# A rarely taken path's DMAs issued from GpSimd instead of SyncE, and another order for four of the last pair's products

## The chip, the cores and the metric

The kernel runs on one core of a Trainium2 chip. The metric is the device time of one execution in microseconds (us). The time is about 1.8 us longer than the span that the profile shows; the span runs from the program's first instruction to its last. A ratio below is the mean time of one kernel's fast runs over the mean of the other's fast runs of the same rounds (in the experiments without the first, profiled run of each), so it is not quite the ratio of the medians that are quoted next to it. Differences between two experiments of the same rounds are differences of the means of six runs each; a "±" behind one is half the width of a 95% interval worked out from the scatter of those runs.

## The reference

```python
def setup_inputs():
    batch, seq, dim, hidden = 16, 256, 512, 2048
    return {
        "x": np.random.randn(batch, seq, dim).astype(np.float32),
        "w1": np.random.randn(dim, hidden * 2).astype(np.float32),
        "w2": np.random.randn(hidden, dim).astype(np.float32),
    }

def reference(x, w1, w2):
    h = x @ w1
    gate, value = np.split(h, 2, axis=-1)
    h = np.maximum(gate, 0) * value
    return (h @ w2).astype(np.float32)
```

## The kernel before

The kernel has two ways. The fast way computes in fp16, with seven products in place of eight (a Strassen-like scheme, P1 to P7), and meanwhile checks that the size of the inputs suits fp16. Only if they do not suit is the general way run afterwards, under a branch. The inputs drawn here suit, so the general way stands in the program but is never executed. Every engine still has to branch over it.

```python
    with ExitStack() as fast:
        unfit = fast_way(fast, tc, x2, w1, w2, out2, flag)
    with tc.If(unfit > 0, label="general"):
        with ExitStack() as general:
            general_way(general, tc, x2, w1, w2, out2)

def general_way(ctx, tc, x2, w1, w2, out2):
    # ... (pools, identity)
    for k in range(NK):
        for j in range(0, 2 * H, 1024):
            t = xp.tile([P, 1024], F32, name="g_t", tag="g_t")
            nc.sync.dma_start(out=t, in_=w1[k * P:(k + 1) * P, j:j + 1024])
            # ... (three more dma_start like it: w2, x, and the output)
```

In the fast way, the second matrix product of the last of four passes is done in pairs of row blocks. The last pair (number 3) is what remains at the very end. Each of its products is eight matmuls. After P1, ScalarE copies the sum from bank X to bank Y. After P5 and P6 it moves W and Y to `pu`; P2 and P4 end in ScalarE copies to the output tile, P7 and P3 in VectorE additions. Each of P2, P7, P3 and P4 of the last pair then sends a quarter of the pair's output, 128 KB, from SyncE.

```python
        def send(self, h, c):
            nc.sync.dma_start(out=out_v[self.s, h, self.t, :, c], in_=self.o[:, h, c])
        # ...
        def P2(self):
            self.o = tmp.tile([P, 2, DO], F32, name="o", tag="tmp")
            nc.scalar.activation(self.o[:, 0, :DO // 2], self.X, COPY, scale=1 / GS)
            if self.end:
                self.send(0, slice(0, DO // 2))
        # ...
        def P4(self):
            nc.scalar.activation(self.o[:, 1, :DO // 2], self.Y, COPY, scale=1 / GS)
            self.send(1, slice(0, DO // 2 if self.end else DO))
    # ...
    LAST_ORDER = ORDER.replace("P5 3, P2 3, P6 3, P3 3, P7 3", "P2 3, P6 3, P5 3, P7 3, P3 3")
    # ... (in the last pass)
            job(84, lambda: tc.mark_branch_hint_location("general", "LikelyTaken", [ENG.PE, ENG.DVE, ENG.SP]))
```

`ORDER` ends in "P1 3, P4 2, P5 3, P2 3, P6 3, P3 3, P7 3, P4 3"; the numeral after the product is the pair.

## Time and profile before

| | before |
|---|---|
| time, median of the first 3 runs | 309.0 us (308.88 to 310.2) |
| span of the profiled run | 307.5 us |
| TensorE busy | 300.7 us, 98% |
| last ScalarE copy begins | 302.97 us |
| last output DMA lands | 305.81 us |
| end of the span | 307.46 us |

From the page of the profile: the span, TensorE's line of the table of busy times, and the chain of work that ended last.

```profile
span 307.5 us, 5285 instructions
...
PE 300.7 (98%) x1905; PEld 184.0 (60%) x1905; DVE 235.9 (77%) x388; ACT 176.4 (57%) x348; POOL 151.4 (49%) x189
...
PE 96%; DMA 1%; SPq 0%; POOL 0%; ACT 0%; issue 0%
```

TensorE is what bounds the kernel. A change that leaves its work alone can only win at the two ends. The end begins as follows (timeline; columns: start us, length us, engine, line, operation, tiles):

```profile
302.97 0.39 ACT L405 ACTIVATE o<-Y 128x256 f32<-128x256 f32 x1 [2.23 <-PE Y L362]
303.38 1.07 SPq L370 DMA_DIRECT2D out_dram<-o  x1
```

The issue of that last output DMA occupies SyncE for 1.07 us; the view of the output tensor for the last three sends (minimum, median and maximum of the issue in ns; then the time from issue to landing) shows that 0.33 us is normal:

```profile
L370 SPq DMA_DIRECT2D out_dram<-o x3: 332/332/1072, 301.7 to 303.4; - x3
...
DMA to landing us min/median/max: 1.7/2.4/2.7
```

The same view for the last send alone:

```profile
DMA to landing us min/median/max: 2.4/2.4/2.4
```

What the sequencers did at the branch over the general way (the view of source line 42; columns: durations in ns, first and last start in us):

```profile
L42 SPq EVENT_SEMAPHORE  x8: 17/17/17, 305.0 to 305.8; - x8
...
L42 PEldq COMPARE_BRANCH  x1: 496/496/496, 301.8 to 301.8; - x1
...
L42 SPq COMPARE_BRANCH  x1: 73/73/73, 304.5 to 304.5; - x1
```

And at the end of the launch (view of source line 785):

```profile
L785 SPq EVENT_SEMAPHORE  x13: 17/28/28, 305.9 to 307.4; - x13
```

So SyncE, which has nothing left to do but wait for its DMAs, runs eight waits after its branch, the eighth held by the last landing at 305.81, and only then starts on the eleven waits of the launch end (the other two of the thirteen belong to the closing barriers). Those eleven take 0.062 us each.

In the 1.2 us from 302.9, the table of DMA queues has an instruction fetch of 16 KB (columns: packets, MB, share of 16 engines' time) among the packets of the output. The records of single packets put its start at 303.06 and its length at 1.01 us:

```profile
q8 instruction: 1, 0.02, 5.3%
```

### The profile page before, as it was taken

The page shows a single profiled execution, that of the slowest core. Times are in us where ns is not written, and L with a number is a line of the kernel's source. Part 1 is how long each engine was busy: PE and PEld are TensorE (multiplying, and loading weights), DVE is VectorE, ACT ScalarE, POOL GpSimd, SP SyncE. Part 2 cuts the span into 40 slices and gives each one's busy share as a digit, 9 for nine tenths or more (in the row PEclk, how much of TensorE's full clock was granted, in tenths as well). Part 3 has the DMA queues.
Part 4 walks back from the last instruction along what each step waited for, and adds up shares of the span by engine and source line. Part 5 has one row for each costly group of instructions (what it writes and reads, how often), then busy time and mean ns, then how long its engine had stood idle before and what let it go on. Part 6 is the DMA issues. An engine that isn't in the chain of part 4 may idle for free.

```text
span 307.5 us, 5285 instructions
## 1 busy us (share of the span) xinstructions
PE 300.7 (98%) x1905; PEld 184.0 (60%) x1905; DVE 235.9 (77%) x388; ACT 176.4 (57%) x348; POOL 151.4 (49%) x189
## 2 busy tenths in 40 slices
PE   7999999999999999999999999999999999999994
PEld 6844444588844444478864444458884444448883
DVE  2579888899768888887438888889536888888841
ACT  2488886455865555538845555546865555553231
POOL 2389999800069899200029889700007998700000
PEclk9999999999999999999999999999999999999998
DMA  6976779964765260001354910000335110001132
GB/s 207 357 257 190 227 177 174 225 123 87 270 193 86 69 136 3 0 0 67 136 175 103 207 34 2 0 2 24 115 108 167 35 34 0 3 1 34 53 120 74
DMA packets 35837, 32.88 MB, mean 107 GB/s; under 512 B 14432, under 2 KB 31328, under 8 KB 35680
## 3 DMA queue, kind: packets, MB, share of 16 engines
q1 hardware_dynamic: 33536, 26.22, 28.0%
q0 software_dynamic: 2272, 6.29, 11.4%
q8 instruction: 16, 0.26, 0.4%
q14 instruction: 13, 0.11, 0.1%
HBM read 27.26 MB, written 12.58 MB: 130 GB/s over the span
## 4 chain that ended last, share of the span: by engine, by line
PE 96%; DMA 1%; SPq 0%; POOL 0%; ACT 0%; issue 0%
PE Y L250 26%; PE X L250 17%; PE W L250 17%; PE Y L362 14%; PE X L362 9%; PE W L362 9%; DMA w_stage<-in_w_dram 1%; PE X L325 1%; PE W L325 1%; PE Y L325 1%; PE Y L498 0%; PE X L498 0%; SPq L488 0%; PE Y L154 0%; POOL w_B L466 0%; ACT o L405 0%
## 5 line engine op out<-in xcount | busy, mean ns | idle before, releaser
L250 PEld LDWEIGHTS <-w_T 128*128 128x128 f16 x496 | 48.3, 98 | 57.3 <-POOL w_T L232 1.1
L179 POOL TENSOR_TENSOR fold<-xh 128x1024 f32<-128x1024 f16 x16 | 30.3, 1894 | 94.5 <-DMA xh<-x 93.7
L250 PE MATMUL X<-x_A,w_B 128*128 128x512 f16 x248 | 73.8, 379 | 0.0
L250 PE MATMUL Y<-x_S,w_T 128*128 128x512 f16 x220 | 65.5, 379 | 0.0
L250 PEld LDWEIGHTS <-w_B 128*128 128x128 f16 x372 | 36.4, 98 | 42.0
L277 DVE SCALAR_TENSOR_TENSOR cc<-W,pu 128x512 f32<-128x512 f32 x62 | 42.9, 691 | 21.2 <-ACT pu L271 20.4
L257 ACT COPY Y<-X 128x512 f32<-128x512 f32 x62 | 35.4, 571 | 38.2 <-PE X L250 37.9
L271 ACT ACTIVATE pu<-Y 128x512 f32<-128x512 f32 x62 | 37.1, 598 | 33.9 <-PE Y L250 32.9
L182 POOL TENSOR_TENSOR fold<-fold 128x512 f32<-128x512 f32 (+2 forms) x96 | 51.8, 539 | 7.5
L362 PEld LDWEIGHTS <-w_stage 128*128 128x128 f16 x512 | 50.0, 98 | 5.8
L287 DVE SCALAR_TENSOR_TENSOR cc<-Y,pu 128x512 f32<-128x512 f32 x62 | 42.9, 691 | 6.7
L282 DVE SCALAR_TENSOR_TENSOR g<-X,cc 128x512 f16<-128x512 f32 x62 | 42.8, 691 | 2.3
L299 DVE SCALAR_TENSOR_TENSOR g<-Y,cc 128x512 f16<-128x512 f32 x62 | 42.2, 681 | 1.8 <-PE Y L250 1.8
L362 PEld LDWEIGHTS <-g 128*128 128x128 f16 x384 | 37.6, 98 | 8.2
L264 ACT ACTIVATE pu<-W 128x512 f32<-128x512 f32 x62 | 37.2, 600 | 0.8 <-PE W L250 0.6
L250 PE MATMUL W<-x_S,w_B 128*128 128x512 f16 x124 | 36.9, 379 | 0.0
L250 PE MATMUL W<-x_S,w_T 128*128 128x512 f16 x124 | 36.9, 379 | 0.0
L250 PE MATMUL Y<-x_A,w_T 128*128 128x512 f16 x124 | 36.9, 379 | 0.0
L362 PE MATMUL X<-w,g 128*128 128x256 f16 x256 | 31.9, 273 | 0.0
L394 DVE SCALAR_TENSOR_TENSOR o<-W,pu 128x256 f32<-128x256 f32 x16 | 6.8, 422 | 19.8 <-PE W L362 19.8
L169 DVE TENSOR_TENSOR w_stage<-g 128x1024 f16<-128x1024 f16 x32 | 21.4, 683 | 0.2
L232 POOL TENSOR_TENSOR w_T<-w_stage 128x512 f16<-128x512 f32 (+1 forms) x16 | 18.7, 1177 | 2.5 <-DMA w_stage<-in_w_dram 2.5
(100 smaller groups left out, 306.2 us busy)
## 6 DMA issues: line engine op xcount, KB each, us to landing
w_stage<-in_w_dram SPq DMA_DIRECT2D x14, 512.0 KB, 6.2
out_dram<-o SPq DMA_DIRECT2D x26, 256.0 KB, 2.1
x<-in_x_dram POOLq DMA_DIRECT2D x4, 1024.0 KB, 9.0
xh<-x SPq DMA_DIRECT2D x16, 256.0 KB, 3.0
w<-in_w_dram POOLq DMA_DIRECT2D x2, 1024.0 KB, 10.2
out_dram<-o SPq DMA_DIRECT2D x12, 128.0 KB, 1.7
w_stage<-in_w_dram SPq DMA_DIRECT2D x4, 256.0 KB, 5.4
x_S<-in_x_dram SPq DMA_DIRECT2D x4, 256.0 KB, 6.1
```

The source lines that it names most:

```text
L169: eng.tensor_tensor(o[n], o[i0], o[i1], op=op)
L179: nc.gpsimd.tensor_tensor(fold, t, t, op=MULT)
L182: nc.gpsimd.tensor_tensor(fold[:, :, :m], fold[:, :, :m], fold[:, :, m:2 * m], op=ADD)
L250: nc.tensor.matmul(ps, wop[wn][:, b, self.jb * P:(self.jb + 1) * P], self.xo[xn][:, b, :], start=fresh and b == 0, stop=b == 1, skip_group ...
L257: nc.scalar.copy(out=self.Y, in_=self.X)
L264: nc.scalar.activation(self.p5, self.W, COPY, scale=GS)
L271: nc.scalar.activation(self.u2, self.Y, COPY, scale=GS)
L277: nc.vector.scalar_tensor_tensor(out=self.c12, in0=self.W, scalar=GS, in1=self.u2, op0=MULT, op1=ADD)
L282: nc.vector.scalar_tensor_tensor(out=self.g[:, self.jb, :TH], in0=self.X, scalar=0.0, in1=self.c12, op0=MAX, op1=MULT)
L287: nc.vector.scalar_tensor_tensor(out=self.c22, in0=self.Y, scalar=GS, in1=self.p5, op0=MULT, op1=ADD)
L299: nc.vector.scalar_tensor_tensor(out=self.g[:, self.jb, TH:], in0=self.Y, scalar=0.0, in1=self.c22, op0=MAX, op1=MULT)
L362: nc.tensor.matmul(ps, self.op[an][:, i], vop[wn][:, i], start=name in ("P1", "P5") and i == 0, stop=i == NJ // 2 - 1, skip_group_check=True)
```

## The change

The diff tells two intents, which I infer. First, if the general way's DMAs belong to GpSimd, the skip path need not raise SyncE's eight DMA semaphores, and SyncE is the engine that ends last. Second, P7's result and its send come earlier, and P2's later, in the last pair. The diff, with the repeated lines of its first part cut:

```diff
-            nc.sync.dma_start(out=t, in_=w1[k * P:(k + 1) * P, j:j + 1024])
+            nc.gpsimd.dma_start(out=t, in_=w1[k * P:(k + 1) * P, j:j + 1024])
 ... (the same in the general way's loads of w2 and x and its store of the output)
@@ class Pair
-            self.s, self.t = s, t
+            self.s, self.t, self.o = s, t, None
+        def outputs(self):
+            if self.o is None:
+                self.o = tmp.tile([P, 2, DO], F32, name="o", tag="tmp")
         def P2(self):
-            self.o = tmp.tile([P, 2, DO], F32, name="o", tag="tmp")
+            self.outputs()
         def P7(self):
+            self.outputs()
@@
-    LAST_ORDER = ORDER.replace("P5 3, P2 3, P6 3, P3 3, P7 3", "P2 3, P6 3, P5 3, P7 3, P3 3")
+    LAST_ORDER = ORDER.replace("P5 3, P2 3, P6 3, P3 3, P7 3", "P6 3, P5 3, P7 3, P2 3, P3 3")
```

## The prediction

> **What bounds the kernel now.** TensorE. The page gives PE 300.7 us busy of a 307.5 us span (98%) at a granted clock of 0.996, and the chain of waits puts 96% of the span on PE. At the end (timeline, and the records of the lines of the branch and of the launch end): the last pair's products run back to back, 0.87 us per eight matmuls, until about 302.9; ScalarE copies P4 to `o` (302.97 to 303.36); SyncE issues the last output DMA at 303.38. That issue takes 1.07 us instead of the usual 0.33, and overlaps a 16 KB instruction fetch at 303.06. It lands at 305.81. SyncE branches at 304.50, goes on at 305.03, and runs eight semaphore waits of the skip path (about 0.08 us each), the eighth held by the landing to 305.83. Then come eleven waits of the launch end, 305.90 to 306.52, 0.062 us each, and two barriers to 307.46.
>
> **What the change does.**
>
> 1. General way. It is not executed with these inputs. But the skip path has to raise every semaphore that the general way would have raised. Before, SyncE does this for its eight DMA semaphores, each after waiting for its own DMA, so the eleven waits of the launch end can't start before the last landing. After (instruction order of the built kernel), SyncE's skip path has none, GpSimd has five instead, and the launch end has twelve waits on SyncE, the last on the last DMA's semaphore. So eleven run while that DMA is in flight, from about 304.7 to 305.4. Saved after the landing: 306.58 (the drain that follows) minus about 305.90, or 0.68 us, all on the critical path.
>
> 2. SyncE's own jump. It now jumps over one instruction instead of 187. The Trainium skill, "Runtime: NRT & Kernel Launch", Instruction fetch mechanics, says that a taken branch to a target outside the fetched window waits for a fetch. The trace agrees in part: 0.46 us after SyncE's branch against 0.13 on ScalarE, which jumps over one instruction. I expect 0.3 us less, hidden under the landing: worth nothing alone. GpSimd's jump gets long instead, at 289.5, 14 us before it matters.
>
> 3. Last pair's order. PE work is the same; P1, P3 and P4 keep their places. P6 moves before P5, and needs Y's copy (296.91 to 297.27) at 297.5: 0.25 us of slack. P7 needs P6's eviction (0.39 us) within P5's 0.87 us. P7's send moves from 301.74 to about 300.9, P2's from 299.0 to about 301.6. P3's and P4's stay at 302.55 and 303.38. Worth 0 to 0.1 us either way.
>
> **Predicted time.** 309.0 - 0.68 = 308.3 us; 8 in 10 between 307.8 and 308.9. Faster by over 2%: 1%; within 2%: 98%; slower: 1%.
>
> **What would show each step.** Step 1: the launch-end waits of SyncE begin near 304.7, the last ends within 0.05 us of the last landing, and the end comes about 1.0 us after it, against 1.65. Step 2: SyncE's first record after its branch comes within 0.2 us. Step 3: no idle PE between the last pair's products; the last issue stays at 303.4 with 1.07 us, if the instruction fetch still falls at 303.06.
>
> **What would make it wrong.** If the last issue were not slowed by the fetch, the landing would come 0.7 us earlier and the gain reach 1.3 us. If another engine's fetch delays the last landing (a fetch made one part of the send at 302.55 land 1 us late), the gain is lost. If the order makes PE wait, it costs some tenths. Run-to-run spread (308.88 to 310.2) is as large as the gain.

## The result, and the profile after

| | before | after |
|---|---|---|
| median of 6 runs | 309.47 us (308.88 to 310.2) | 308.99 us (308.08 to 309.99) |
| ratio | 1 | 0.9984, 95% interval 0.9959 to 1.0009 |
| start of last copy to end of span | 4.49 us | 4.33 us |
| start of last copy to last landing | 2.84 us | 3.37 us |
| last landing to end of span | 1.65 us | 0.96 us |

The measured time is 0.09 us above the predicted range. The difference is 0.48 us of medians where 0.68 was predicted, and it is not clear of noise. The same lines of the changed kernel, page first:

```profile
span 307.6 us, 5283 instructions
...
PE 301.0 (98%) x1905; PEld 183.9 (60%) x1905; DVE 235.9 (77%) x388; ACT 176.3 (57%) x348; POOL 151.3 (49%) x189
...
PE 96%; DMA 2%; SPq 1%; issue 0%; ACT 0%
```

The timeline of the end, and the last four sends in the view of the output tensor:

```profile
303.26 0.38 ACT L410 ACTIVATE o<-Y 128x256 f32<-128x256 f32 x1 [1.36 <-PE Y L362]
303.67 0.33 SPq L374 DMA_DIRECT2D out_dram<-o  x1
```

```profile
L374 SPq DMA_DIRECT2D out_dram<-o x4: 332/332/332, 301.2 to 303.7; - x4
...
DMA to landing us min/median/max: 1.7/2.3/3.5
```

The 3.5 us belong to the send before the last, which also landed before the last did (at 306.32). The view for the last send alone, and the instruction fetch in the table of DMA queues from 303.4 to 305.4:

```profile
DMA to landing us min/median/max: 3.0/3.0/3.0
```

```profile
q8 instruction: 1, 0.02, 4.6%
```

The branch (line 42) and the launch end (now line 790):

```profile
L42 POOLq EVENT_SEMAPHORE  x5: 17/43/43, 290.3 to 290.6; - x5
...
L42 PEldq COMPARE_BRANCH  x1: 1736/1736/1736, 301.2 to 301.2; - x1
...
L42 SPq COMPARE_BRANCH  x1: 68/68/68, 304.1 to 304.1; - x1
```

```profile
L790 SPq EVENT_SEMAPHORE  x14: 17/28/28, 304.3 to 307.5; - x14
```

What was meant to happen did. SyncE has no wait on line 42, its launch-end waits begin at 304.3 instead of 305.9, and the end comes 0.96 us after the landing instead of 1.65.

But 0.53 us of this was given back: the last landing came later after the copy. The last issue is no longer slow (0.33 us), yet the DMA lands 2.96 us after it. Its sixteen parts, read from the semaphore's updates: fourteen between 305.18 and 305.34, one at 305.62, one at 306.63. The Trainium skill, "DMA: Bandwidth & Descriptors", Why a DMA increments its semaphore by 16 and not by 1, says that a DMA's parts finish independently on up to 16 engines and that only the full 16 means that all data landed. The trace agrees: the wait ended at 306.64, with the sixteenth. By the packet records a 16 KB instruction fetch began at 303.66 (before: 303.06), within 0.01 us of the last issue, and took 1.46 us.

And TensorE's branch, which the prediction had left out, began at 301.21 instead of 301.79, although the last copy was 0.29 us later, and took 1.74 us instead of 0.50.

### The profile page after: what moved, and what is told of

Its sections match the earlier page's. It is cut to its first block, busy times and chain, and to the rows that moved or that the text cites. A ratio compares the mean times of both kernels' runs of the same rounds, so it can differ in the third digit from the quotient of the medians.

```text
span 307.6 us, 5283 instructions
## 1 busy us (share of the span) xinstructions
PE 301.0 (98%) x1905; PEld 183.9 (60%) x1905; DVE 235.9 (77%) x388; ACT 176.3 (57%) x348; POOL 151.3 (49%) x189
## 4 chain that ended last, share of the span: by engine, by line
PE 96%; DMA 2%; SPq 1%; issue 0%; ACT 0%
PE Y L250 26%; PE X L250 17%; PE W L250 17%; PE Y L362 14%; PE W L362 9%; PE X L362 9%; DMA x_S<-in_x_dram 2%; PE X L325 1%; PE W L325 1%; PE Y L325 1%; SPq L493 0%; PE Y L503 0%; SPq L217 0%; PE X L503 0%; ACT o L410 0%
```

## The experiments

Theory A: the saved waits are the gain; the new order spoils part of it, because it moves TensorE's branch and the instruction fetch behind the branch onto the last output DMA. Theory B: the order does nothing and where the fetch falls is chance. Four rounds of experiments were made on three chips; times of "before" of the same rounds are given with each round.

All traces together first. Times are us from the start of the last ScalarE copy, read from the records of single instructions, packets and semaphore updates; "fetch 1" and "fetch 2" are starts of the last 16 KB fetches before and after TensorE's branch begins.

| kernel | TensorE's branch: start, length | fetch 1 | fetch 2 | last issue | last landing | end |
|---|---|---|---|---|---|---|
| before | -1.18, 0.50 | -4.60 | 0.09 | 1.07 | 2.84 | 4.49 |
| e13 before again | -1.18, 0.50 | -4.45 | 0.07 | 1.15 | 2.93 | 4.58 |
| e1 general way only | -1.18, 0.50 | -4.08 | 0.09 | 1.00 | 2.79 | 3.75 |
| e12 the same again | -1.17, 0.50 | -4.04 | 0.07 | 0.97 | 2.75 | 3.72 |
| after | -2.05, 1.74 | -3.00 | 0.40 | 0.33 | 3.37 | 4.33 |
| e3 after again | -2.05, 1.58 | -2.99 | 0.25 | 0.33 | 3.11 | 4.07 |
| e10 after, third | -2.05, 1.96 | -2.65 | 0.62 | 0.33 | 3.43 | 4.40 |
| e2 order only | -2.05, 1.84 | -3.00 | 0.50 | 0.33 | 3.41 | 5.06 |
| e14 the same again | -2.06, 1.70 | -2.72 | 0.37 | 0.33 | 3.06 | 4.71 |
| e4 after, short general way | -2.05, 1.80 | -2.95 | 0.50 | 0.34 | 2.99 | 3.95 |
| e5 after, shifted by 62 | -2.06, 0.41 | -6.58 | -0.71 | 0.48 | 2.46 | 3.43 |
| e9 the same again | -2.05, 0.42 | -6.69 | -0.71 | 0.33 | 2.11 | 3.07 |
| e15 order only, shifted by 62 | -2.05, 0.41 | -6.63 | -0.71 | 0.56 | 2.41 | 4.06 |
| e6 general way only, shifted by 62 | -1.18, 0.41 | -6.65 | 0.17 | 0.33 | 2.92 | 3.88 |
| e7 general way only, shifted by 217 | -1.18, 4.44 | none near | -0.15, 3.99 | 1.76 | 3.64 | 4.60 |
| e8 no branch | none | -4.68 | none | 0.33 | 2.11 | 3.07 |
| e11 e5 without TensorE's hint | -2.05, 3.52 | -6.66 | -1.05, 2.20 | 0.39 | 2.37 | 3.33 |

### First round: the parts alone, and a shorter jump

Before: mean of 11 runs 309.37 us, median 309.4.

**e1**, only the general way's DMAs from GpSimd:

```diff
-            nc.sync.dma_start(out=t, in_=w1[k * P:(k + 1) * P, j:j + 1024])
+            nc.gpsimd.dma_start(out=t, in_=w1[k * P:(k + 1) * P, j:j + 1024])
 ... (and the other three)
```

> Only the general way's DMAs from GpSimd; the last pair keeps its old order. Theory A (the saved waits are the whole gain, the new order spoils part of it by moving TensorE's branch and its 16 KB instruction fetch onto the last output DMA): the span ends 0.95 to 1.0 us after the last landing (before 1.65), the last landing 2.8 to 2.9 us after the start of the last ScalarE copy, and the time is 0.6 to 0.8 us below before, ratio about 0.9978. Theory B (the order does nothing; where the fetch falls is chance): same end, the landing anywhere between 2.4 and 3.4 us after the copy, the time 0.4 to 0.7 us below before and the same as the full change within 0.3 us.

Measured: median 308.22 us, mean 308.20, ratio 0.996 (0.9942 to 0.9978). The end came 0.96 us after the landing, and the landing 2.79 us after the copy, both as theory A had it. The gain in time, 1.16 us, is larger than either theory had it and than the 0.74 us that the trace shows at the end (4.49 to 3.75); the repetition e12 below gives 0.66.

**e2**, only the new order:

```diff
-    LAST_ORDER = ORDER.replace("P5 3, P2 3, P6 3, P3 3, P7 3", "P2 3, P6 3, P5 3, P7 3, P3 3")
+    LAST_ORDER = ORDER.replace("P5 3, P2 3, P6 3, P3 3, P7 3", "P6 3, P5 3, P7 3, P2 3, P3 3")
 ... (and the helper `outputs`)
```

> Only the last pair's new order; the general way's DMAs stay on SyncE. Theory A: the branch of TensorE and the fetch that follows it fall as in the changed kernel (branch begun 0.6 us earlier than before and taking over 1 us, the fetch beginning within 0.1 us of the last issue), one part of the last DMA lands 1 us late, and the time is 0.3 to 0.6 us above before, ratio about 1.0015. Theory B: the time is that of before within 0.3 us, ratio 0.999 to 1.001. In both, the end comes 1.65 us after the last landing.

Measured: median 309.34 us, mean 309.36, ratio 0.9998 (0.9981 to 1.0016). The trace is theory A's in every point (branch, fetch, landing 3.41, end 5.06), but the time is theory B's. This was the one contradiction left, and e14 and e15 were made for it.

**e3**, the changed kernel again, without an edit:

> The changed kernel once more, as the partner of the other three and for a second trace. Theory A: the 16 KB fetch at TensorE's branch falls again within 0.1 us of the last issue and one part lands about 1 us late (last landing 3.3 us after the start of the last copy); time 0.3 to 0.6 us above the kernel with the general way's DMAs moved alone. Theory B: the fetch falls elsewhere by some tenths, and the landing changes with it; same time as the kernel with the DMAs moved alone. Both: 0.4 to 0.7 us below before.

Measured: median 308.62 us, mean 308.80, ratio 0.9982 (0.9964 to 1.0). In the same rounds e1 was faster by 0.60 ± 0.40 us. The full change is slower than half of it. The fetch began 0.17 us before the last issue rather than within 0.1, and the landing was 3.11.

**e4**, a general way with one chunk in place of eight, so that TensorE jumps over some 210 instructions instead of 1698:

```diff
-    for c in range(T // TH):
+    for c in range(1):
```

> The changed kernel, with a general way that handles one chunk of eight only (never executed here, wrong for inputs that need it): TensorE jumps over some 210 instructions instead of 1698, and VectorE over fewer too. If the fetches at the branch are what delays the last DMA, they move or vanish, the last landing comes 2.1 to 2.4 us after the start of the last copy instead of 3.37, and the time falls 0.4 to 1.0 us below the full change. If the length of the jump does not matter, nothing changes (within 0.2 us).

Measured: median 309.01 us, mean 308.96, ratio 0.9985 (0.9967 to 1.0004); against e3 no gain. The fetch after the branch was still there, at 0.50. So the length of the jump is not what matters here, and this guess was a miss.

### Second round: moving the fetch without touching the order

In e1 to e4 the order and the time of the fetch change together. The two fetches come from TensorE's instruction stream. The Trainium skill, "Runtime: NRT & Kernel Launch", Instruction fetch mechanics, says that instructions are refilled in blocks of 16 KiB, or 256 instructions, and that the next block is fetched while the current one executes. The traces agree: the fetches on queue 8 are of 16384 bytes, and the shifts below moved them. So empty instructions in TensorE's stream, spread over the kernel, move the block boundaries and leave the order of products and sends as it is.

Before: mean of 11 runs 309.54 us, median 309.24.

**e5**, the changed kernel with one empty instruction after the first product of each of the 62 blocks:

```diff
             self.mm("P1", self.X, True)
+            for _ in range(1):
+                nc.tensor.nop(hint="shift", nofuse=True)
```

> The changed kernel with 62 empty instructions in TensorE's stream (one after each first product of a block), which move its last instruction-block boundary 62 instructions earlier. Fetch theory (in the new order TensorE enters its last block so late, at 3.0 us before the last copy, that its branch waits 1.44 us after that fetch and the next fetch falls on the last output DMA): the first fetch begins 4 us or more before the copy, the branch takes about 0.5 us instead of 1.6 to 1.8, the second fetch begins at about -0.8 us, the last issue takes 0.33 us and the last landing comes 2.1 to 2.5 us after the start of the copy instead of 3.1 to 3.4; time 0.6 to 1.2 us below the full change and 0.2 to 0.7 below the general-way-only kernel, 307.5 to 308.0. Rival (the late landing belongs to the new order of the output DMAs, not to the fetch): landing stays at 3.1 or more and the time at 308.7 to 309.

Measured: median 307.9 us, mean 307.97, ratio 0.9944 (0.9924 to 0.9964). With the order of products and sends unchanged, the branch took 0.41 us, fetch 2 came at -0.71, and the landing at 2.46 us (the last issue took 0.48 us where 0.33 was expected). The rival, that the order of the sends makes the landing late, falls.

**e6**, the control: the same edit to e1.

> Control: the same 62 empty instructions in the kernel with only the general way's DMAs moved (old order). The branch there already takes 0.50 us, so both theories expect no change: branch at -1.18 us, second fetch at 0.1, last issue about 1.0 us, landing 2.8, time 308.0 to 308.4. If the empty instructions themselves cost or gain time, it shows here.

Measured: median 308.61 us, mean 308.57, ratio 0.9965 (0.9944 to 0.9986). A near miss in two points: fetch 2 came 0.1 us later than in e1, so the last issue was not slowed, but one part of the DMA landed late instead (2.92). The time is a little above the expected range. The empty instructions as such show no gain (e1 had 308.20, though in the round before and not side by side). One thing more can be read here: e5 and e6 have the same shift and differ in the order alone, and e5 is faster by 0.60 ± 0.49 us (from copy to end 3.43 against 3.88). With fetch 1 early in both, at -6.6, the new order is the better one, because its branch comes 0.87 us earlier and fetch 2 with it (-0.71 against 0.17).

**e7**, the old order with 217 empty instructions (three after each P1, one more after P5 of every other block), which is 39 short of a whole block of 256:

```diff
             self.mm("P1", self.X, True)
+            for _ in range(3):
+                nc.tensor.nop(hint="shift", nofuse=True)
 ...
             self.mm("P5", self.W, True)
+            if self.jb % 2:
+                nc.tensor.nop(hint="shift", nofuse=True)
```

> Old order, general way's DMAs moved, with 217 empty instructions, which is 39 short of a block of 256: the last block boundary falls later than in the old order without them. Fetch theory: the harm of the new order appears without it: first fetch at -3.2 to -2.1 us, the branch takes over 0.7 us and ends about 1.44 us after that fetch, the second fetch falls at or after the last issue (0.2 to 1.2 us), that issue takes 0.33 us and one part lands late, last landing 2.9 to 3.5 us after the copy; time 0.2 to 0.7 us above the general-way-only kernel. Rival (the order of the DMAs does it): landing 2.8, same time as the general-way-only kernel.

Measured: median 308.97 us, mean 309.03, ratio 0.9981 (0.996 to 1.0003), which is 0.46 ± 0.51 us above e6 of the same rounds. The harm appeared at the end of the trace in the old order, but not by the way that was expected, and the times alone do not resolve it. No fetch began in the 14 us before the branch; the branch's own fetch began at -0.15 us, and the branch took 4.44 us (view of line 42):

```profile
L42 PEldq COMPARE_BRANCH  x1: 4444/4444/4444, 301.5 to 301.5; - x1
```

The last issue did not take 0.33 us, as expected, but 1.76: that fetch was in flight when the issue began, and the issue ended 0.33 us after the fetch did. The landing was at 3.64 us.

**e8**, the old order without the general way and its branch (right for these inputs only):

```diff
-        unfit = fast_way(fast, tc, x2, w1, w2, out2, flag)
-    with tc.If(unfit > 0, label="general"):
-        with ExitStack() as general:
-            general_way(general, tc, x2, w1, w2, out2)
+        fast_way(fast, tc, x2, w1, w2, out2, flag)
 ...
-            job(84, lambda: tc.mark_branch_hint_location("general", "LikelyTaken", [ENG.PE, ENG.DVE, ENG.SP]))
```

> Old order, without the general way and its branch (right for these inputs only): what the branch costs in all. Fetch theory: only one fetch of TensorE in the last 6 us, the last issue takes 0.33 us, landing 2.1 to 2.3 us after the copy, end 0.95 us later; time 0.5 to 0.8 us below the general-way-only kernel, 307.4 to 307.7. If fetches do not matter, landing 2.8 and the same time as the general-way-only kernel.

Measured: median 307.6 us, mean 307.51, ratio 0.9931 (0.991 to 0.9952), 1.06 ± 0.51 us below e6 of the same rounds. One fetch in the last 6 us, the last issue 0.33 us, the landing at 2.11: as expected; the gain in time is larger than expected. The end came 3.07 us after the copy, against 3.88 in e6 and 3.75 in e1: the difference is what the general way's branch costs at the end in all.

### Third round: side by side on another chip, and the hint

Before: mean of 11 runs 308.93 us, median 308.91.

**e9**, e5 again:

> The kernel with the new order and 62 empty instructions once more, on one chip with the full change and with the general-way-only kernel, to compare them in the same rounds. Fetch theory: branch 0.4 us, second fetch at about -0.7 us, last landing 2.1 to 2.5 us after the copy; time 0.5 to 1.0 us below the full change and 0.1 to 0.5 us below the general-way-only kernel. Rival (the earlier gain was chance of the start of the kernel): the three within 0.3 us of each other.

Measured: median 307.7 us, mean 307.76, ratio 0.9967 (0.9949 to 0.9984). It is 0.94 ± 0.51 us below the changed kernel (e10) and 0.51 ± 0.60 us below e12, at the upper end of the first expected range and at the edge of the second. The view of line 42, the timeline of the last issue, and the output tensor's view for it:

```profile
L42 PEldq COMPARE_BRANCH  x1: 416/416/416, 300.3 to 300.3; - x1
```

```profile
302.74 0.33 SPq L376 DMA_DIRECT2D out_dram<-o  x1
```

```profile
DMA to landing us min/median/max: 1.7/1.7/1.7
```

The last send lands 1.7 us after its issue; the changed kernel's took 2.96 us, the one of before 2.4.

**e10**, the changed kernel, third time:

> The changed kernel, partner of the other three. Fetch theory: branch 1.6 to 1.8 us, ending 1.44 us after the end of the fetch that begins at -3.0; second fetch at 0.25 to 0.5; last landing 3.0 to 3.4; time 0.3 to 0.7 us below before. Rival (chance): landing anywhere from 2.1 to 3.4.

Measured: median 308.73 us, mean 308.70, ratio 0.9996 (0.9979 to 1.0013). Fetch 1 came 0.35 us later than in the first two traces, at -2.65, outside the expectation; the branch was longer with it (1.96 us) and ended, again, 1.44 us after the end of that fetch. Fetch 2 (0.62) and the landing (3.43) were just outside the expected ranges too, and the mean is 0.23 us below before where 0.3 to 0.7 was expected.

**e11**, e5 without the branch hint for TensorE:

```diff
-            job(84, lambda: tc.mark_branch_hint_location("general", "LikelyTaken", [ENG.PE, ENG.DVE, ENG.SP]))
+            job(84, lambda: tc.mark_branch_hint_location("general", "LikelyTaken", [ENG.DVE, ENG.SP]))
```

> New order, 62 empty instructions, and no branch hint for TensorE (VectorE and SyncE keep theirs). If the hint is what brings the fetch of the branch's target ahead of the branch, the fetch now begins only after the branch does (at -1.9 to -0.9 us), the branch takes 2.5 to 4.5 us, as it did where the last block came too late (4.44 us), and the fetch after it falls at +1.5 us or later, when the last DMA has nearly landed: landing 2.1 to 2.4, time equal to or up to 0.3 us below the kernel with the hint. If the hint does nothing, branch 0.4 us and all as with the hint.

Measured: median 308.27 us, mean 308.12, ratio 0.9972 (0.9956 to 0.9989). The branch became long as expected (view of line 42):

```profile
L42 PEldq COMPARE_BRANCH  x1: 3515/3515/3515, 301.3 to 301.3; - x1
```

A fetch began only after the branch had, at -1.05 us, and a further one at 2.20. The expected gain did not come: the fetch at -1.05 lengthened the issue of the send before the last (0.75 us), the landing was 2.37, and the mean is 0.36 ± 0.50 us above e9. The hint shortens the branch, but what it is worth in time is not resolved; even without it this kernel was 0.58 ± 0.43 us faster than e10 of the same rounds.

**e12**, e1 again:

> Only the general way's DMAs moved, once more, partner in the same rounds. Fetch theory: branch 0.50 us, second fetch at 0.1 to 0.2, landing 2.8 to 2.9, end 0.96 us later; time 0.2 to 0.6 us below the full change. Rival (the order does nothing): same time as the full change within 0.2 us.

Measured: median 308.23 us, mean 308.27, ratio 0.9979 (0.996 to 0.9998), 0.43 ± 0.55 us below e10. Together with e1 against e3, the mean of the two differences is 0.51 us, in the same direction both times.

### Fourth round: the order alone

Before: mean of 11 runs 309.27 us, median 309.31, on a third chip.

**e13**, the kernel before, for a second trace:

> The kernel before, for a second trace. Fetch theory: branch at -1.18 us with 0.50 us, second fetch at about 0.1, last issue 1.0 us, landing 2.8 us after the start of the last copy, end 1.65 us after the landing: 4.4 to 4.5 us from copy to end. If its landing varies as much as in the new order (up to 3.4), that explains why the order alone timed the same.

Measured: median 309.25 us, mean 309.20, ratio 0.9996 (0.9984 to 1.0008). The end is the same within 0.1 us as in the first trace. In the old order the landing came at 2.75 to 2.93 us in four traces (before, e13, e1, e12), in the new order at 3.06 to 3.43 in five (after, e3, e10, e2, e14).

**e14**, the order alone again (the edit of e2):

> Only the new order, once more. Fetch theory: branch 1.6 to 2.0 us, second fetch 0.25 to 0.6, landing 3.0 to 3.5, 4.7 to 5.1 us from copy to end; time 0.3 to 0.6 us above before in the same rounds. Rival: same time as before within 0.2 us, again.

Measured: median 309.49 us, mean 309.47, ratio 1.0012 (0.9996 to 1.0027): 0.20 us above before, at the edge of the rival. The trace is theory A's again, 4.71 us from copy to end against 4.58 for e13.

**e15**, the order alone, with the 62 empty instructions of e5:

> The new order with the general way's DMAs on SyncE, and 62 empty instructions in TensorE's stream. Fetch theory: branch 0.4 us, second fetch at -0.7, landing 2.1 to 2.5, end 1.65 us after it: 3.75 to 4.15 us from copy to end; time 0.6 to 1.2 us below the order alone and 0.3 to 0.7 us below before. Rival (the fetch does not matter without the GpSimd move): the three within 0.3 us.

Measured: median 308.98 us, mean 308.90, ratio 0.9991 (0.9979 to 1.0003). It is 0.57 ± 0.63 us below e14, just under the expected range, and 0.37 us below before; from copy to end 4.06 us. The branch, the fetch and the landing moved as in e5, without the move to GpSimd. What the new order costs alone is small, 0.35 us by the mean of two traces of each (4.89 against 4.54) and 0.0 and 0.2 us by the two sets of times; the times alone do not resolve it.

### What follows

Theory A stands in the traces and in the times of e5, e9 and e10, with one correction: what spoils the new order is not that TensorE's branch begins earlier, but that the fetch before it (fetch 1) comes later. The chain of it, each link with its numbers:

1. TensorE reaches its branch 0.08 us after VectorE's addition for P7 ends (before: 301.71, branch 301.79; after: 301.13, branch 301.21), because P4, the last product, waits for that addition, and the branch stands behind P4 in the stream. The new order ends this addition 0.87 us earlier before the last copy.
2. If the fetch of a block is then not long done, the branch does not finish until 1.42 to 1.44 us after the end of that fetch. That holds for all eight traces with a long branch (after, e2, e3, e4, e7, e10, e11, e14), whichever fetch it was; in the eight with a short branch, that moment lay before the branch began. In the new order this made the branch 1.6 to 2.0 us long, and it ended at -0.48 to -0.09 us, later than in the old order (-0.69), although it had begun earlier. By this link it would have ended no earlier had it begun at -1.18.
3. The next 16 KB fetch begins 0.7 to 0.95 us after the branch ends, in every trace with a branch, whatever the length of the jump.
4. That fetch took 0.9 to 1.5 us. Where it met the last output DMA, either the issue was held (0.97 to 1.15 us instead of 0.33: before, e1, e12, e13; it ended 0.28 to 0.38 us after the fetch did), or one of the sixteen parts landed 0.8 to 1.3 us after the fourteenth (after, e2, e3, e4, e6, e10, e14; it landed 1.3 to 1.5 us after the fetch's end). If it begins at -0.71 us, it is over or nearly over in time (issues of 0.33 to 0.56 us), and without a branch it does not exist; the last send then lands at 2.1 to 2.5 us.

Another queue's instruction fetch, of 8 KB on queue 14, also began 0.3 to 0.8 us after the copy in every trace but e8's. It is not what made the sixteenth part late: in e9 it ran from 0.34 to 0.85 us, through the last issue, and the landing came at 2.11.

Left open: why fetch 1 came at -3.0 to -2.65 in the new order and at -4.6 to -4.0 in the old one, though TensorE has the same number of instructions in both. TensorE's waits stand at other places of the stream in the new order, which can hold its sequencer back before the boundary. The traces fit that: the first matmul of P7 waits for ScalarE's move after P6, whose semaphore came at -3.97 in the new order, 1.0 to 1.3 us before fetch 1, and at -3.10 in the old order, after fetch 1 had begun. But no run isolates it. Open too is what decides whether a fetch that meets a send does harm: in six traces of the new order P7's send was issued at -2.10 while fetch 1 was in flight, took 0.33 us and landed 1.7 us later. That the late part is on the very DMA engine that serves the fetch is also inferred from the times; the trace does not name the engine of a packet.

The best version is e5 (e9): the full change plus a shift of TensorE's block boundary, 307.7 us against 308.73 for the change and 308.91 for before in the same rounds.

## Why the prediction was wrong

**Step 1, the general way: right.** Predicted: launch-end waits of SyncE from near 304.7, the end about 1.0 us after the last landing, 0.68 us saved. Measured: from 304.3, 0.96 us after, 0.69 us saved (1.65 minus 0.96) in every pair of traces. Alone (e1, e12) the move gained 1.16 and 0.66 us in time, 0.80 us by the mean of two traces each.

**Step 2, the jumps: right.** SyncE's first record after its branch came 0.14 us after the branch's end (0.46 before), and GpSimd's five waits and its longer jump were over by 291.0.

**Step 3, the order: this is the step that failed.** The prediction said "Worth 0 to 0.1 us either way" and "the last issue stays at 303.4 with 1.07 us, if the instruction fetch still falls at 303.06". It had checked all the data waits of TensorE's matmuls, correctly: there is no idle time between the products, and from the hundred-and-first matmul to the last copy every traced kernel took 289.6 us within 0.06. It had treated TensorE as done with its last matmul. But TensorE's sequencer has still a branch to make, and the path that the sum left out runs over it: in the new order fetch 1 came 1.0 us or more later, the branch was held until 1.4 us after that fetch ended, and the fetch behind the branch began at 0.25 to 0.62 us after the start of the last copy instead of 0.07 to 0.09. There it no longer lengthened the last issue (0.33 us in place of the predicted 1.07) but made one part of the last DMA land late, 2.96 us after the issue instead of 2.43. In place of 0 to 0.1 us, this term cost 0.53 us in the trace, and 0.60 ± 0.40 and 0.43 ± 0.55 us in the timed pairs with the move to GpSimd; with the order alone it was 0.35 us in the traces and not resolved by the times. Of the list of what would make the prediction wrong, one item was close: a fetch that delays the last landing; but it named "another engine's fetch" and let the chance of it not enter the sum.

**The base.** The prediction subtracted its saving from a median of three runs, 309.0. With six runs it was 309.47, and the means of the other rounds lay between 308.93 and 309.54. The 0.09 us by which the range was missed is smaller than this error. The two errors do not cancel: the base too low by 0.47 us and the order's cost of 0.53 us missing in the sum both make the prediction too low, and with both mended it would be 309.3 us. The measured 308.99 is 0.3 us below that, well within the scatter of six runs against six (about ± 0.8 us by the interval of the ratio), so that the miss was small is partly luck. Most of the scatter is made in the first 14 us: the hundred-and-first matmul began between 12.56 and 13.77 us in the seventeen traces, with no relation to the experiment that I can see.

## What to carry to other kernels

A path that is never executed still costs at its branch: look at which engine has to make up for its semaphores, and give that work to an engine that is finished early. When the order of the last instructions is changed, check not only the data waits but also when each sequencer reaches its branch and where its instruction fetches fall, since here a fetch that met the last output DMA held its issue or made a part of it land late. A gain found by such an alignment is fragile, because instructions added to the stream move it (62 did so here); compare in the same rounds and read the last microseconds of the trace.

## What the Trainium skill lacked or had wrong

- "Runtime: NRT & Kernel Launch", Instruction fetch mechanics, calls the cost of crossing a 16 KiB block "mostly hidden", and no page gives what a data DMA loses to such a fetch. Here a fetch in flight lengthened the issue of an output DMA from 0.33 to 0.97 to 1.76 us, or made the last of its sixteen parts land 0.8 to 1.3 us after the fourteenth.
- The same section says that a taken branch to a target that was not fetched stalls, but has no duration of the stall and no word of the fetch that follows. Measured on TensorE: 0.41 to 0.50 us when the fetch had ended 1.9 us or more before the branch began, 3.52 and 4.44 us when it began after the branch, and always a further 16 KB fetch 0.7 to 0.95 us after the branch's end.
- The same section calls prefetch "purely sequential". With a branch hint for TensorE the branch took 0.41 us and no fetch came between the one at -6.6 and the branch; with the hint removed it took 3.52 us with a fetch of its own (e9, e11). So the hint seems to bring the target's block ahead of the branch; the trace does not show which block a fetch brings. No page mentions the hint.
- The same section gives refills in 16 KiB blocks without distinction of engines. The fetches on queue 14, which did not move when TensorE's stream was shifted, were of 8192 bytes; those on queue 8, which moved, were of 16384.
- No page says that a skipped path leaves semaphore waits behind at its branch: eight on SyncE here, 0.07 to 0.10 us apart where they did not have to wait for a landing.
